# Three loads of x in an output projection, asked for earlier in SyncE's queue

## Chip, cores and metric

The kernel runs on one core of a Trainium2 chip. What is measured is the device time of one execution in microseconds. Engines are named as in the profile: PE is TensorE's matmuls, DVE is VectorE, ACT is ScalarE, POOL is GpSimd, SP is SyncE, which issues most of the DMAs.

## What is computed

One layer of a trunk, for a sequence of 512 tokens and a width of 2048, all in float32. Cut to what matters:

```python
hn = rmsnorm(x, norm_g)
y  = swa_mixer(hn, ...)               # q, k, v, gate = hn @ w_in; attention in a window of 128
                                      # returns (out * silu(gate)) @ w_out   <- the output projection
x  = x + y
g  = sigmoid(rmsnorm(x, ple_norm) @ ple_gate)
x  = x + (p @ ple_proj) * g
return rmsnorm(x, final_g)
```

## The kernel before

**Stages.** The kernel first makes the norm, the keys, the values and the first queries, then projects the remaining queries and gates while attention runs block by block, then does the output projection (`w_out`, 2048 x 2048), and last the projection by `ple_gate` with the final norm and the stores. Every float32 product is made of three matmuls on split operands (`mm3`, L126 to L128): high times high, low times high, high times low, where a high part is a cast (`fp32r`) and a low part is what the cast left over.

**The output projection** is done in Strassen-like products of quarters of the matrices. `ORDER_OUT = (1, 7, 6, 5, 3, 4)` gives the order of the six large products (the seventh is replaced by products half their size, the `small` ones). Each product `p` has two halves `jj`, for the two column blocks of 512; each half is one call of `unit` and has four steps, and a step takes one weight piece of 128 x 1024 (512 KB) and makes 2 x 2 x 3 = 12 matmuls of 128 x 512 with it. Products 1, 6, 5 and 3 add up in the same PSUM banks, so that product 1's result has to be taken out before product 6 goes on in them.

A step looks like this: `unit` gets its piece, issues its matmuls, runs some of the work queued in `later` (adds of finished products to x), then calls `todo`, which is where loads of x are asked for:

```python
def load_x(j, queue):                                                    # L1015
    queue.dma_start(x1[j], a["x"].rearrange("(t p) d -> p t d", p=P)[:, :, j * 512 : (j + 1) * 512])
...
for m in range(4):                                                       # in unit
    bh, bl = B.get(at[p, jj][m])
    ...                                                                  # 12 matmuls
    some_later(4 - m)
    todo()
...
def todo():                                                              # in the loop over ORDER_OUT
    step = next(calls)
    part = x_at.get((p, jj, step))
    if part is not None:
        load_x(part, nc.sync)
    next(nxt, None)
```

**x.** `x1s` is a tile of 128 x 4 x 4 x 512, and `x1[j]` is its part for the columns from 512 j on: 1 MB each, in rows of 2 KB (a weight piece's rows have 4 KB). Part 0 is loaded by POOL's queue just ahead of the projection; parts 2, 1 and 3 are asked for on SP's queue at the places that `x_at` names as (product, half, step): part. The tile lies in room that attention used, so the first load from each queue waits for attention's last product on PE. `add_to_x` (L1054 adds, L1056 subtracts) takes a block of 128 x 512 from PSUM and needs the x part there: product 1's halves go to parts 0 and 1, product 7's first half to parts 2 and 0, its second half to 3 and 1. Product 1's two results are held back (`waiting`) into product 7's first and product 6's first half, ahead of product 6's next use of the same banks.

**Weight pieces.** `Pieces` (the object `B`) holds the order of all pieces of this projection and the next. `ahead` asks for a piece three or four pieces before its turn (`_prepare`, L747, on SP's queue) and splits it two before its turn: the cast on ACT (L754, `bhi`) and the subtraction on DVE (L755, `blo`). A piece goes into one of three buffers (tag `wraw`), and so its load waits on SP until DVE has split the piece three before it. From product 6 on (`far_from` to `far_to`) pieces go instead into a pool of eight buffers and are asked for six pieces ahead, so that they enter SP's queue among the last pieces of product 7. The split parts have three buffers too, so that a cast waits until PE has let go of the piece three before it.

**Forms.** The activations' quarters are added, subtracted and split for the next product while the present one runs (`steps`, one step at each `todo`): `gate<-gate,gate` at L855 on DVE, `fho` at L862 and L867 on ACT, `flo` at L863 and L868 on DVE. They read the gates, not x.

**Order.** On PE and SP instructions stand in the order of the program. On DVE, ACT and POOL, in this stage, a scheduler orders them when the kernel is built, by its own estimate of when each can run. Each queue then runs strictly in order: an instruction that waits holds up all that stand behind it on its engine. SP's queue carries every load named here except x's part 0.

Of the kernel before, what the change touches and what calls it, by code (L numbers as in the profile page):

```python
# [55 lines left out]
def trunk_kernel(ctx: ExitStack, tc: tile.TileContext, a: dict):  # L56
# [958 lines left out]
    def load_x(j, queue):  # L1015
        queue.dma_start(x1[j], a["x"].rearrange("(t p) d -> p t d", p=P)[:, :, j * 512 : (j + 1) * 512])
# [128 lines left out]


    load_x(0, nc.gpsimd)
    x_at = {(1, 1, 1): 2, (7, 0, 1): 1, (7, 0, 3): 3}
    waiting = {(7, 0): (1, 0), (6, 0): (1, 1)}
    held = {}  # L1150
    for n, p in enumerate(ORDER_OUT):
# [386 lines left out]
```

## Time and profile before

| | |
|---|---|
| timed runs | 791.11, 791.59, 791.53 us; median 791.53 us |
| profiled execution | 792.39 us, its span 790.7 us |
| granted clock of TensorE | 0.998 |
| instructions | 11096 |
| loads of x: 3 on SP's queue, 1 on POOL's | 1024.0 KB each, issued at 462.55, 473.49, 479.71 us (SP) and 450.94 us (POOL) |
| loads of weight pieces of the projection from `in_w_out` and `w_out` on SP's queue | 22 + 32 of 512.0 KB |
| projection's first large product begins | 450.82 us |

Times inside an execution are in microseconds from the span's start. A row of the timeline gives start, length, engine, source line, operation, tiles (written <- read) and, in brackets, how long the engine stood idle before it and what ended that. The length of a DMA's row is the time to issue it; its transfer ends at the landing, which the view of DMA issues tells. A row of the windows gives, for a stretch, its length, busy time and instructions of PE, PE's weight loads, DVE, ACT and POOL, then the granted clock, the busy share of the 16 DMA engines and GB/s. A row of the waits gives total us, times and the longest.

### The profile page before, as it was taken

The numbers are of one execution on the slowest core, as the hardware profiler recorded it, in microseconds if no ns is written. First come the engines' busy times: TensorE is split into PE (matmuls) and PEld (weight loads), VectorE is DVE, ScalarE is ACT, GpSimd is POOL, SyncE is SP. The second block draws the span as 40 slices with busy tenths as digits, with TensorE's granted clock in tenths as the row PEclk, the third lists the DMA queues.
The fourth block names the chain that finished last, engine by engine and source line by source line (L and its number), as shares of the span: only waits on it lengthen the run. The fifth ranks groups of instructions, "written<-read, shape, count | busy, mean of one in ns | idle before, by whom it ended". The sixth has DMA issues, their size and how long they took to land. (4 is left out here: it accounts for less than half of the span.)

```text
span 790.7 us, 11096 instructions
## 1 busy us (share of the span) xinstructions
PE 779.7 (99%) x3726; PEld 652.3 (82%) x3726; DVE 607.9 (77%) x1038; ACT 506.5 (64%) x1064; POOL 137.5 (17%) x256
## 2 busy tenths in 40 slices
PE   9999999999999999999999999999999999999995
PEld 8888888888888888888888887888888888888885
DVE  4537697877878687877777897778779589877996
ACT  6733586666767576766657753457689766656953
POOL 0201423131223223122222100000000022202000
PEclk9999999999999999999999999999999999999999
DMA  9988999999999989999997579667873799989723
GB/s 348 277 216 297 194 269 300 291 289 260 282 273 262 271 238 306 263 280 262 281 270 188 142 262 377 234 210 227 269 278 101 278 300 268 240 236 253 213 96 118
DMA packets 47817, 198.07 MB, mean 251 GB/s; under 512 B 7104, under 2 KB 8128, under 8 KB 42000
## 3 DMA queue, kind: packets, MB, share of 16 engines
q1 hardware_dynamic: 38736, 151.95, 55.7%
q0 software_dynamic: 9024, 45.41, 29.6%
q8 instruction: 29, 0.48, 0.2%
q14 instruction: 28, 0.23, 0.1%
HBM read 189.16 MB, written 71.35 MB: 329 GB/s over the span
## 5 line engine op out<-in xcount | busy, mean ns | idle before, releaser
L755 DVE TENSOR_TENSOR blo<-braw,bhi 128x1024 fp32r<-128x1024 f32 x108 | 131.2, 1221 | 38.4 <-ACT bhi L754 37.6
L754 ACT CAST bhi<-braw 128x1024 fp32r<-128x1024 f32 x108 | 113.2, 1051 | 58.3 <-PE o L128 25.2
L126 PE MATMUL gps<-xh,whi 128*128 128x512 f32 x256 | 100.0, 390 | 0.0
L127 PE MATMUL gps<-xl,whi 128*128 128x512 f32 x256 | 99.9, 390 | 0.0
L128 PE MATMUL gps<-xh,wlo 128*128 128x512 f32 x256 | 99.7, 390 | 0.0
L126 PE MATMUL qps<-xh,whi 128*128 128x512 f32 x224 | 87.8, 392 | 0.0
L127 PE MATMUL qps<-xl,whi 128*128 128x512 f32 x224 | 87.4, 390 | 0.0
L128 PE MATMUL qps<-xh,wlo 128*128 128x512 f32 x224 | 87.3, 390 | 0.0
L110 DVE TENSOR_TENSOR wlo<-wraw,whi 128x1024 fp32r<-128x1024 f32 x60 | 73.5, 1227 | 3.8 <-ACT whi L109 3.6
L126 PE MATMUL o<-bhi,fho 128*128 128x512 f32 x192 | 74.9, 390 | 1.1 <-ACT bhi L754 1.1
L127 PE MATMUL o<-blo,fho 128*128 128x512 f32 x192 | 74.9, 390 | 0.8 <-DVE blo L755 0.8
L570 POOL TENSOR_SCALAR_AFFINE_SELECT own<-r 64x512 fp32r<-64x512 f32 (+1 forms) x48 | 32.4, 675 | 244.1 <-DVE r L560 240.1
L128 PE MATMUL o<-bhi,flo 128*128 128x512 f32 x192 | 74.8, 390 | 0.0
L556 ACT CAST r<-pt 128x256 fp32r<-128x256 f32 x64 | 23.9, 374 | 68.9 <-PE pt L551 68.6
L109 ACT CAST whi<-wraw 128x1024 fp32r<-128x1024 f32 x60 | 62.3, 1039 | 5.5 <-issue 4.1
L126 PE MATMUL g<-bhi,fhg 128*128 128x512 f32 x160 | 62.8, 392 | 0.0
L128 PE MATMUL g<-bhi,flg 128*128 128x512 f32 x160 | 62.3, 389 | 0.0
L127 PE MATMUL g<-blo,fhg 128*128 128x512 f32 x160 | 62.3, 389 | 0.0
L128 PEld LDWEIGHTS gps<-xh,wlo 128*128 128x128 f32 x256 | 48.1, 188 | 10.3
L126 PEld LDWEIGHTS gps<-xh,whi 128*128 128x128 f32 x256 | 48.1, 188 | 9.2
L127 PEld LDWEIGHTS gps<-xl,whi 128*128 128x128 f32 x256 | 48.1, 188 | 8.8
L529 ACT ACTIVATE t<-t,sm 128x129 f32<-128x129 f32 (+1 forms) x128 | 49.6, 389 | 8.7 <-DVE sm L525 7.4
(241 smaller groups left out, 1761.6 us busy)
## 6 DMA issues: line engine op xcount, KB each, us to landing
wraw<-in_w_gate_in SPq DMA_DIRECT2D x32, 512.0 KB, 8.1
w_out<-in_w_out POOLq DMA_DIRECT2D x32, 512.0 KB, 9.1
braw<-w_out SPq DMA_DIRECT2D x32, 512.0 KB, 4.7
wraw<-in_w_q SPq DMA_DIRECT2D x28, 512.0 KB, 6.6
braw<-in_w_out SPq DMA_DIRECT2D x22, 512.0 KB, 3.9
braw<-in_ple_gate SPq DMA_DIRECT2D x22, 512.0 KB, 5.5
xw<-in_first SPq DMA_DIRECT2D x14, 640.5 KB, 6.6
w_out<-in_w_out SPq DMA_DIRECT2D x16, 512.0 KB, 10.5
```

The costliest lines, as they stand in the source:

```text
L109: nc.scalar.copy(hi, raw)
L110: nc.vector.tensor_sub(lo, raw, hi.bitcast(F32))
L126: nc.tensor.matmul(ps, sh, mh, start=first, stop=False, skip_group_check=more)
L127: nc.tensor.matmul(ps, sh, ml, start=False, stop=False, skip_group_check=more)
L128: nc.tensor.matmul(ps, sl, mh, start=False, stop=last, skip_group_check=more)
L529: nc.scalar.activation(su, su, AF.Exp, bias=sm[:, u : u + 1], accum_out=sm[:, 2 + u : 3 + u])
L556: nc.scalar.copy(rh, src)
L570: nc.gpsimd.affine_select(out=flat(own), in_=flat(r).bitcast(F32), pattern=[[0, 8], [sign, HB]], compare_op=ALU.is_ge, fill=0.0, base=-HB ...
L754: nc.scalar.copy(hi, raw)
L755: nc.vector.tensor_sub(lo, raw, hi.bitcast(F32))
```

## The change

The places at which x's parts are asked for. Part 2 moves from the second step of product 1's second half to the last step of its first half; part 1 from the second step of product 7's first half to the second step of product 1's second half; part 3 from the fourth step of product 7's first half to the first step of the same half. Nothing else in the source is touched; the scheduler orders some instructions of DVE and ACT anew.

```diff
     load_x(0, nc.gpsimd)
-    x_at = {(1, 1, 1): 2, (7, 0, 1): 1, (7, 0, 3): 3}
+    x_at = {(1, 0, 3): 2, (1, 1, 1): 1, (7, 0, 0): 3}
     waiting = {(7, 0): (1, 0), (6, 0): (1, 1)}
```

## The prediction

> **What bounds the kernel now.** The page comes first, then the view of waits kept to PE, then PE's timeline around the wait that it names.
>
> ```profile
> span 790.7 us, 11096 instructions
> PE 779.7 (99%) x3726; PEld 652.3 (82%) x3726; DVE 607.9 (77%) x1038; ACT 506.5 (64%) x1064; POOL 137.5 (17%) x256
> ```
> ```profile
> PE o L126 <- ACT bhi L754: 1.1, 1, 1.1
> ...
> PE o L127 <- DVE blo L755: 0.8, 1, 0.8
> ```
> ```profile
> 782.51 0.39 DVE L1225 TENSOR_TENSOR s<-e,s 128x224 f32<-128x224 f32 x1 [1.15 <-PE e L128]
> ```
>
> TensorE is busy from its first to its last instruction. Behind its end stands only a tail that starts from its last product (the last row: VectorE waits for PE). In the whole span PE waits for another engine twice, both times in the output projection (tile `o`), once each for the two halves of a split weight piece. So the time can fall by little more than these waits, and any new wait of PE is paid in full. Where they stand:
>
> ```profile
> 450.82 0.40 PE L126 MATMUL o<-bhi,fho 128*128 128x512 f32 x1
> ...
> 472.84 0.39 PE L127 MATMUL o<-blo,fho 128*128 128x512 f32 x1
> ...
> 483.49 0.39 PE L126 MATMUL o<-bhi,fho 128*128 128x512 f32 x1
> ...
> 492.94 0.50 PE L126 MATMUL o<-bhi,fho 128*128 128x512 f32 x1 [1.09 <-ACT bhi L754]
> 494.20 0.50 PE L127 MATMUL o<-blo,fho 128*128 128x512 f32 x1 [0.76 <-DVE blo L755]
> ...
> 496.86 0.39 PE L126 MATMUL o<-bhi,fho 128*128 128x512 f32 x1
> ```
>
> I number the weight pieces of the projection from 0: product 1 uses 0 to 7, product 7 uses 8 to 15, product 6 starts with 16. Piece 0 begins at 450.82 and piece 12 at 483.49, so a piece costs PE 32.67 / 12 = 2.7225 us. Without a wait piece 15 would begin at 483.49 + 3 x 2.7225 = 491.66 and piece 16 at 494.38. They begin at 492.94 and 496.86. The loss is 496.86 - 494.38 = 2.48 us, all of it at piece 15 (the two waits, 1.09 and 0.76, leave out the refilling of the matmul pipe around them).
>
> Why piece 15 was late is read from the queue of SP, the landings and the two engines that split a piece:
>
> ```profile
> 425.56 34.07 SPq L747 DMA_DIRECT2D braw<-in_w_out  x8
> 462.18 0.33 SPq L747 DMA_DIRECT2D braw<-w_out  x1
> 462.55 0.43 SPq L1016 DMA_DIRECT2D x1s<-in_x  x1
> 465.64 7.80 SPq L747 DMA_DIRECT2D braw<-w_out  x4
> 473.49 0.43 SPq L1016 DMA_DIRECT2D x1s<-in_x  x1
> 476.00 3.67 SPq L747 DMA_DIRECT2D braw<-w_out  x4
> 479.71 0.43 SPq L1016 DMA_DIRECT2D x1s<-in_x  x1
> 483.21 13.55 SPq L747 DMA_DIRECT2D braw<-w_out  x9
> ```
> ```profile
> 481.36 0.69 DVE L1056 TENSOR_TENSOR x1s<-x1s,o 128x512 f32<-128x512 f32 x1 [1.91 <-DMA x1s<-in_x]
> 481.96 1.22 DVE L755 TENSOR_TENSOR blo<-braw,bhi 128x1024 fp32r<-128x1024 f32 x1
> ```
> ```profile
> 478.74 1.05 ACT L754 CAST bhi<-braw 128x1024 fp32r<-128x1024 f32 x1 [2.15 <-DMA braw<-w_out]
> ...
> 491.84 2.94 ACT L754 CAST bhi<-braw 128x1024 fp32r<-128x1024 f32 x3 [2.31 <-DMA braw<-w_out]
> ```
>
> The first of the nine at 483.21 is piece 15. It goes into one of three raw buffers and waits until DVE has split piece 12, which ends at 481.96 + 1.22 = 483.18. That split stood behind an add to x (L1056), for which DVE waited 1.91 us until x's second part had landed. Then the load itself is slow. In the views of DMA issues kept to one issue each (at 457.57, 462.55, 465.64, 473.49, 479.71 and 483.21; KB and us to landing at the end):
>
> ```profile
> braw<-in_w_out SPq DMA_DIRECT2D x1, 512.0 KB, 3.3
> ```
> ```profile
> x1s<-in_x SPq DMA_DIRECT2D x1, 1024.0 KB, 5.8
> ```
> ```profile
> braw<-w_out SPq DMA_DIRECT2D x1, 512.0 KB, 4.0
> ```
> ```profile
> x1s<-in_x SPq DMA_DIRECT2D x1, 1024.0 KB, 7.8
> ```
> ```profile
> x1s<-in_x SPq DMA_DIRECT2D x1, 1024.0 KB, 10.8
> ```
> ```profile
> braw<-w_out SPq DMA_DIRECT2D x1, 512.0 KB, 8.5
> ```
>
> Piece 15 takes 8.5 us where a piece alone takes 3.3, and lands at 491.7; its cast starts at 491.84 and PE gets it at 492.94. The windows, one for each half product, say why (DMA share and GB/s at the end):
>
> ```profile
> 461.70:472.60 10.90, 10.90 (x49) 9.01 (x48) 10.90 (x13) 5.80 (x8) 0.00 (x0) 1.00 0.77 271
> 472.60:483.50 10.90, 10.90 (x50) 9.02 (x49) 8.99 (x11) 4.46 (x5) 0.00 (x0) 1.00 0.94 333
> 483.50:494.40 10.90, 9.05 (x39) 6.96 (x38) 7.81 (x11) 5.01 (x7) 0.00 (x0) 1.00 1.03 406
> ```
>
> In the last one the 16 DMA engines are full at 406 GB/s; in the first they are not. At 406 GB/s one part of x (1.05 MB) costs 2.6 us and a piece (0.52 MB) 1.3 us. A piece alone takes 3.3, so 2.0 us of a load are latency.
>
> **The change, part by part.** The number of instructions stays; no engine gets an operation more. Three issues move up SP's queue. In the built order they stand so (pieces by number, x parts by column index): before `8, x2, 9, 10, 11, 12, x1, 13, 16, 14, 17, x3, 15, 18...`; after `6, x2, 7, 8, x1, 9, 10, 11, x3, 12, 13, 16, 14, 17, 15, 18...`.
>
> ```profile
> 457.57 0.33 SPq L747 DMA_DIRECT2D braw<-in_w_out  x1
> ```
> ```profile
> 471.39 0.32 SPq L747 DMA_DIRECT2D braw<-w_out  x1
> ```
>
> *x2* follows piece 6 (457.57): asked for at 457.9, not 462.55. It is the first of the three to enter room that attention used; the last attention product ended just ahead of 450.82, where the projection begins, so SP has nothing to wait for there. *x1* follows piece 8 (462.18): 462.55, not 473.49. *x3* follows piece 11 (471.39): 471.8, not 479.71. An issue itself costs 0.43 us of SP, which mostly waits for buffers: nothing.
>
> *What now stands behind an x.* Piece 7 follows x2, pieces 8 and 9 follow x2 and x1. Moving data from 457.57 + 2.0 = 459.6 on, at the full rate, pieces 6, x2 and 7 (2.1 MB, 5.2 us) are in by 464.8, then 8 by 466.1, x1 by 468.7 and 9 by 470.0. The row of 4.0 us at 465.64 is the same case in the trace: piece 9, 3.1 us behind an x part, landed 0.7 us later than a piece alone, at 469.6. What the landings may cost is read from DVE, which is full in this stretch (10.90 of 10.90 us):
>
> ```profile
> 470.14 1.22 DVE L755 TENSOR_TENSOR blo<-braw,bhi 128x1024 fp32r<-128x1024 f32 x1
> ...
> 471.88 1.21 DVE L755 TENSOR_TENSOR blo<-braw,bhi 128x1024 fp32r<-128x1024 f32 x1
> 473.02 1.22 DVE L855 TENSOR_TENSOR gate<-gate,gate 128x1024 f32<-128x1024 f32 x1
> ```
>
> These are the splits of pieces 8 and 9 and a form's subtraction. Piece 8 is ready at 471.36, PE's use of its low half is at 472.84: 1.5 us to spare. Its cast (1.05 us) must start by 469.1 to keep DVE's slot; landing at 466.1 leaves 3 us. Cost: nothing, cover 3 us.
>
> *The scheduler's order on DVE.* Built with the new order, the subtraction (L855) goes ahead of piece 9's split, and the two adds of product 1's second half (L1056) go ahead of piece 11's. Piece 9's split moves from 471.88 to about 473.0 and ends at 474.2; PE needs it at 450.82 + 9 x 2.72 + 0.23 = 475.5. 1.3 us are left, so nothing is paid. Piece 12 waits for that buffer: its issue slips from about 473.1 to 474.3, behind x3. Piece 11, x3 and 12 are 2.1 MB or 5.2 us from 473.4: piece 12 lands at 478.6, as now (its cast began at 478.74).
>
> *The wait that goes.* The adds need x1, which lands by 469 instead of 481.3 (473.49 + 7.8). DVE's 1.91 us wait goes. DVE was free for piece 12 at 481.36 - 1.91 = 479.45; with both adds now ahead of it (0.60 us apart by the rows at 481.36 and 481.96) it is split from 480.65 to 481.87, and piece 15 is asked for 1.3 us earlier, at 481.9. In front of it in the queue only pieces 14 and 17 are still moving (1.05 MB, 2.6 us), no x: it lands by about 485.2, the time of a piece alone. Its cast cannot begin before PE has let go of piece 12's buffer at 486.2; cast and split then end at about 488.7, 3 us ahead of its use at 491.9. Next late is nothing: behind 496.86 PE waits nowhere, and each later load there is released by a split that moves with PE.
>
> The sum: -2.48 us, nothing added. The profiled execution took 792.39 us (its span 790.7), and would take 789.9; the timed runs have a median of 791.53, 0.86 less, and give 791.53 - 2.48 = **789.05**. If all of those 0.86 us lay in this stall, the timed runs lose only 1.6 there and the result is 789.9; 788.7 if the timed runs scatter downwards as they do now (0.4 us).
>
> **The rivals.** 0.2% is 1.58 us, about what a measurement can tell from no change: from 789.95 to 793.11.
>
> *Part of the stall stays.* Right behind piece 15 SP asks for eight pieces far ahead (18 on). If the engines share their time between loads instead of serving them in order, these still slow it, and it gains only its 1.3 us of earlier issue: a stall of 1.2 us is left, 790.25. Against: in the full stretch x3, asked for at 479.71, landed at 490.5 and piece 15, 3.5 us behind it in the queue, 1.2 us later, one piece's time. Chance 0.13.
>
> *The change doesn't reach it.* The burst alone makes the stall, x or not: 791.5. Against: 1.05 MB less in a stretch that moved 406 x 10.9 = 4.4 MB. Chance 0.05.
>
> *Slower: x ahead of weights in the tight stretch.* Place: piece 9, behind x2 and x1. From 459.6 on 4.2 MB must be in by 473.1 (cast and split 2.3 us, use at 475.5), which takes 311 GB/s; below that PE waits. The trace shows 271 in that stretch. At 271 piece 9 lands at 475.1, it is split by 477.4 and PE loses 1.9 us; x3 takes 3.9 us at that rate, of which pieces 9 to 11 win back 3 x 0.8 (1.9 us each against PE's 2.72), so that piece 12 costs 1.5 more; and with the queue then as full as now at 491 the old stall stays: 791.53 + 3.4 = 794.9. For it: x's rows are shorter in memory than a piece's. Against: 271 was what was asked for (share 0.77), and the 406 came with an x part in flight. The Trainium skill, "DMA: Bandwidth & Descriptors", section "Queues, rings and completion order", says that each DMA engine takes a ring's descriptors in order, and that completion all the same isn't first in, first out. By that a piece behind an x waits out all of it (2.6 us), as in my sum; the 4.0 us row agrees, being late and not overtaking. Chance 0.09.
>
> **How the numbers follow.** Stall gone 0.73 (788.7 to 789.9), part of it 0.13, no effect 0.05, slower 0.09. The range 788.7 to 791.0 takes in the first two. Faster 0.73, same 0.13 + 0.05 = 0.18, slower 0.09.
>
> **What would show it.** Right: no wait of PE at piece 15, piece 16 beginning near 494.4, no wait of DVE for x at L1056, landings under 5 us for piece 15. Wrong: a PE wait between 464 and 484 at piece 7, 8, 9 or 12 (x in front of weights), or piece 15's cast still beginning after 489.

## The result, and the profile after

| | before | changed |
|---|---|---|
| timed runs, median | 791.27 us (790.53 to 792.31, 18 runs) | 789.87 us (789.61 to 790.63, 18 runs) |
| ratio | | 0.9983, 95% interval 0.9976 to 0.9991 |
| profiled execution, its span | 792.39 us, 790.7 | 790.63 us, 788.9 |

The changed kernel is faster by 0.17%, 1.4 us in the medians, where 2.48 us were forecast (789.05; range 788.7 to 791.0). That is a little less than the 0.2% that the prediction took as the least to be told from no change; the interval does not reach 1, so the gain is told from none all the same. The ratios here and below are on record with their intervals; they are not the quotients of the medians and can differ from these by up to 0.001. The profile after, the page and then the waits of PE:

```profile
span 788.9 us, 11095 instructions
PE 779.8 (99%) x3726; PEld 652.7 (83%) x3726; DVE 608.1 (77%) x1038; ACT 507.1 (64%) x1064; POOL 138.8 (18%) x256
```
```profile
PE warm_ps L141 <- PEq L1528: 0.8, 1, 0.8
```

Both waits in the projection are gone; the one left is the program's start. In PE's timeline these are the first matmuls of pieces 0, 15 and 16:

```profile
451.35 0.40 PE L126 MATMUL o<-bhi,fho 128*128 128x512 f32 x1
...
492.17 0.39 PE L126 MATMUL o<-bhi,fho 128*128 128x512 f32 x1
...
494.89 0.39 PE L126 MATMUL o<-bhi,fho 128*128 128x512 f32 x1
```

From piece 0 to piece 16 it is 494.89 - 451.35 = 43.54 us, before 496.86 - 450.82 = 46.04: in these two executions 2.50 us came from exactly where the prediction put 2.48. The spans differ by only 1.8 because this execution reached the projection 0.53 us later, in code that the change doesn't touch, and took 294.0 instead of 293.8 us behind piece 16.

How the loads now stand in SP's queue; then, on DVE, the split of piece 9, the two adds and the split of piece 12; then, on ACT, the casts of pieces 12 and 15:

```profile
458.46 0.43 SPq L1016 DMA_DIRECT2D x1s<-in_x  x1
459.82 0.33 SPq L747 DMA_DIRECT2D braw<-in_w_out  x1
462.69 0.33 SPq L747 DMA_DIRECT2D braw<-w_out  x1
463.07 0.43 SPq L1016 DMA_DIRECT2D x1s<-in_x  x1
466.16 6.07 SPq L747 DMA_DIRECT2D braw<-w_out  x3
472.28 0.43 SPq L1016 DMA_DIRECT2D x1s<-in_x  x1
```
```profile
473.53 1.22 DVE L755 TENSOR_TENSOR blo<-braw,bhi 128x1024 fp32r<-128x1024 f32 x1
...
476.40 1.28 DVE L1056 TENSOR_TENSOR x1s<-x1s,o 128x512 f32<-128x512 f32 x2
...
481.55 1.23 DVE L755 TENSOR_TENSOR blo<-braw,bhi 128x1024 fp32r<-128x1024 f32 x1 [0.39 <-ACT bhi L754]
```
```profile
480.46 1.06 ACT L754 CAST bhi<-braw 128x1024 fp32r<-128x1024 f32 x1 [2.90 <-DMA braw<-w_out]
...
488.77 1.05 ACT L754 CAST bhi<-braw 128x1024 fp32r<-128x1024 f32 x1 [1.44 <-DMA braw<-w_out]
```

The two adds no longer wait; piece 12 is split late only because its own load landed late; piece 15's cast still waits for its load, but at 488.77 and not at 491.84. The loads of piece 9 (issued at 466.16) and piece 15 (at 482.81), each from the view of DMA issues kept to that one:

```profile
braw<-w_out SPq DMA_DIRECT2D x1, 512.0 KB, 5.9
```

Both took 5.9 us, 9 instead of 4.0 and 15 instead of 8.5. (The load of piece 9 varies by itself: in two more profiles of the kernel before, taken below, it took 5.2 and 5.9 us.) The windows show the full stretch spread over the three half products:

```profile
461.70:472.60 10.90, 10.90 (x50) 9.03 (x49) 10.90 (x13) 5.37 (x7) 0.00 (x0) 1.00 0.93 351
472.60:483.50 10.90, 10.90 (x50) 9.03 (x49) 10.31 (x12) 5.26 (x6) 0.00 (x0) 1.00 0.98 351
483.50:494.40 10.90, 10.90 (x49) 9.03 (x49) 9.13 (x12) 5.76 (x7) 0.00 (x0) 1.00 0.99 377
```

271, 333 and 406 GB/s have become 351, 351 and 377.

### The profile page after: what moved, and what is told of

It is laid out like the page before. It is cut to its first block, busy times and chain, and to the rows that moved or that the text cites. A ratio compares the mean times of both kernels' runs of the same rounds, so it can differ in the third digit from the quotient of the medians.

```text
span 788.9 us, 11095 instructions
## 1 busy us (share of the span) xinstructions
PE 779.8 (99%) x3726; PEld 652.7 (83%) x3726; DVE 608.1 (77%) x1038; ACT 507.1 (64%) x1064; POOL 138.8 (18%) x256
## 5 line engine op out<-in xcount | busy, mean ns | idle before, releaser
L560 DVE TENSOR_TENSOR r<-pt,r 128x256 fp32r<-128x256 f32 x56 | 23.7, 423 | 41.0 <-ACT r L556 40.4
```

Source lines behind the costliest of these rows:

```text
L560: nc.vector.tensor_sub(rl, src, rh.bitcast(F32))
```

## The experiments

Two questions were open. Which of the two things that the prediction took together made piece 15 late: that it was asked for late, behind adds that waited for x's part 1, or that part 3's megabyte stood in front of it? And why do the medians differ by 1.4 us when the profiles show 2.5 us of wait? Each experiment stands beside runs of the kernel before on its own chip; there were three such chips, on which the kernel before has medians of 791.1, 790.49 and 790.9 us.

**The kernel before, profiled again (`b_again`, `b_third`).** No edit.

> The kernel before, unchanged, for a second profile. Open is why the profiles differ by 2.5 us at piece 15 while the medians differ by 1.4 us. Theory A (the wait differs from execution to execution and the first profile caught a long one): the wait at piece 15 is again there but of another size, anywhere from 0.5 to 2.5 us, and the span moves with it. Theory B (the wait is always 2.5 us, and the changed kernel loses 1.1 us somewhere else): 2.4 to 2.6 us again, span 790.5 to 791.

> The kernel before, unchanged, for a third profile: the first had 2.5 us of loss at piece 15, the second 1.9. If the wait differs from execution to execution, a third value between 0.5 and 2.5; if it is a matter of the profile alone, 1.9 to 2.5 again.

PE at piece 15 in the second and in the third profile:

```profile
492.69 0.49 PE L126 MATMUL o<-bhi,fho 128*128 128x512 f32 x1 [0.56 <-ACT bhi L754]
493.95 0.50 PE L127 MATMUL o<-blo,fho 128*128 128x512 f32 x1 [0.77 <-DVE blo L755]
```
```profile
491.53 0.50 PE L126 MATMUL o<-bhi,fho 128*128 128x512 f32 x1
492.79 0.50 PE L127 MATMUL o<-blo,fho 128*128 128x512 f32 x1 [0.76 <-DVE blo L755]
```

Measured as in the prediction, against the pitch of pieces 0 to 12, the loss is 1.9 us in the second (span 790.4) and 1.3 us in the third (span 789.3), 2.5 in the first. The wait is there in all three and each time of another size, and the three spans follow it. The runs of the kernel before spread from 789.87 to 793.24 us over all comparisons here; a part of that is not the wait, since the projection itself began between 450.47 and 451.35 us in the profiles of all kernels. So the gain isn't a constant of the change either, but the size of a wait that differs from execution to execution.

The landings tell where the difference arises. They are counted here from piece 0's first matmul. Piece 17, the last load in front of part 3, landed after 36.95, 36.40 and 35.78 us in the three profiles, and piece 15 after 40.94, 40.37 and 39.76, each time 4.0 us later: 2.7 for part 3 and 1.3 for itself. The loss is in all three the landing of piece 15 less 38.46 us, within 0.03 us. So the price of part 3 is the same each time; what differs is how far the queue has come by then. Why that differs is not shown.

**Part 1 alone (`x1_alone`).**

```diff
-    x_at = {(1, 1, 1): 2, (7, 0, 1): 1, (7, 0, 3): 3}
+    x_at = {(1, 1, 1): 2, (1, 1, 2): 1, (7, 0, 3): 3}
```

> Only part 1 moves: asked for right behind piece 9 (466.0 instead of 473.5), so that the two adds do not wait for it; part 3 stays in the queue in front of piece 15. If the late asking for piece 15 (behind the adds that waited for part 1) is what counts, the wait at piece 15 falls to 0 to 0.5 us and the time to that of the changed kernel (ratio 0.998 to 0.9985). If the megabyte of part 3 in front of piece 15 is what counts, at least 1.2 us of the wait stay and the ratio is 0.9992 or more.

791.65 us against 791.1, ratio 1.0008 (0.9999 to 1.0016). The adds no longer wait for part 1, and piece 15 is asked for at 481.71, 1.5 us before the time in the first profile. It gains nothing by it:

```profile
braw<-w_out SPq DMA_DIRECT2D x1, 512.0 KB, 10.4
```

It took 10.4 us instead of 8.5 and landed at 492.1 (before: 491.7), since part 3 was still ahead of it and the engines were full. In this full queue, asking earlier was not landing earlier. The edit did one thing more, though: in DVE's new order the two adds stand ahead of piece 10's split, so that piece 13, which goes into that buffer, was asked for at 477.70 instead of 476.00 (1.2 us later, counted from piece 0), and the DMA engines were not full in the stretch before:

```profile
472.60:483.50 10.90, 10.90 (x50) 9.03 (x49) 10.34 (x12) 4.84 (x5) 0.00 (x0) 1.00 0.80 261
```

So this run shows that the earlier asking doesn't suffice, and not what part 1's megabyte is worth. In this execution the wait was also followed by something that the prediction did not know of, told at the end.

**Part 3 alone, moved back (`x3_behind`).**

```diff
-    x_at = {(1, 1, 1): 2, (7, 0, 1): 1, (7, 0, 3): 3}
+    x_at = {(1, 1, 1): 2, (7, 0, 1): 1, (7, 1, 0): 3}
```

> Only part 3 moves, and it moves back, not forward: behind pieces 15 and 18 in SP's queue. The adds wait for part 1 as before (1.9 us) and piece 15 is asked for at 483.2 as before; DVE's order is that of before. If the megabyte in front of piece 15 counts, it lands 2.6 us earlier, near 489.2, and the wait at piece 15 falls to 0 to 0.4 us (ratio 0.998 to 0.9987). If the late asking counts, most of the wait stays: over 1.2 us, ratio 0.9992 or more.

790.07 us against 791.1, ratio 0.9983 (0.9974 to 0.9992): the same ratio as the change, with parts 1 and 2 at their old places. DVE's order is that of before up to piece 14's split; piece 15's split then stands one step earlier, ahead of a form's low part. That can't have made the gain, as in the kernel before DVE stood idle for 2.2 us ahead of piece 15's split. PE waits nowhere in the projection. The adds still wait for part 1, if less than in the first profile (0.8 us instead of 1.9), and piece 15 is asked for at 482.58. Counted from piece 0 that is 1.1 us earlier than in the first profile, and 0.9 us later than in `x1_alone`, where the earlier asking gained nothing. Here are the add, the load of piece 15 (asked for at 482.58) and its cast:

```profile
480.73 0.69 DVE L1056 TENSOR_TENSOR x1s<-x1s,o 128x512 f32<-128x512 f32 x1 [0.81 <-DMA x1s<-in_x]
```
```profile
braw<-w_out SPq DMA_DIRECT2D x1, 512.0 KB, 5.1
```
```profile
487.82 1.05 ACT L754 CAST bhi<-braw 128x1024 fp32r<-128x1024 f32 x1 [0.54 <-DMA braw<-w_out]
```

It landed at 487.7, now 1.3 us behind piece 17 and not 4.0. Its cast begins at 487.82, 1 us before that of the changed kernel. The megabyte in front of piece 15 decides.

**Part 3 alone, moved forward (`x3_alone`).**

```diff
-    x_at = {(1, 1, 1): 2, (7, 0, 1): 1, (7, 0, 3): 3}
+    x_at = {(1, 1, 1): 2, (7, 0, 0): 3, (7, 0, 1): 1}
```

> Only part 3 moves forward, behind piece 11 as in the changed kernel; parts 2 and 1 stay. No x is left between pieces 14 and 15 in the queue, but part 1 now stands behind part 3 and piece 12 and should land near 483.5; the two adds, which DVE here has behind piece 12's split, wait for it and hold up piece 13's split. Theory 'the bytes in front of piece 15': no wait at piece 15; a small one of 0.3 to 0.8 us at piece 13; ratio 0.9985 to 0.9995. Theory 'the late asking behind the adds': the adds wait longer than before, so the wait at piece 15 stays or grows; ratio 1.000 or more.

790.01 us against 790.49, ratio 0.9993 (0.9984 to 1.0002): the times alone don't tell this from no change. The profile has no wait of PE, at 13 neither: part 1 landed at 481.5, two us sooner than expected, and DVE waited 0.3 us for it. But piece 15 has almost nothing in hand:

```profile
490.67 2.36 DVE L755 TENSOR_TENSOR blo<-braw,bhi 128x1024 fp32r<-128x1024 f32 x2 [0.25 <-ACT bhi L754]
```

The first of the two is piece 15's split. It ends at 490.67 + 1.22 = 491.9, and PE uses it at 492.1, 0.2 us later. With part 3 forward and parts 2 and 1 where they were, the engines are full from 472.6 on (390 GB/s, then 408), and everything behind is just in time. The other two moves, into the stretch with room, bring the reserve of the changed kernel, 1.3 us in its first profile and 1.9 in a second one (`a_again`).

**Part 2 alone (`x2_alone`).**

```diff
-    x_at = {(1, 1, 1): 2, (7, 0, 1): 1, (7, 0, 3): 3}
+    x_at = {(1, 0, 3): 2, (7, 0, 1): 1, (7, 0, 3): 3}
```

> Only part 2 moves, into a stretch in which the DMA engines have time, and far ahead of the full stretch. Expected by both theories: nothing, the wait at piece 15 stays at 1.3 to 2.5 us; ratio 0.9993 to 1.0007. If the part of the gain that the prediction could not place lies with part 2, the ratio is 0.999 or less.

790.61 us against 790.49, ratio 0.9997 (0.9988 to 1.0006). No gain that could be measured; but the times on this chip could hardly have shown one, as `x3_alone`, in whose profile PE's wait is gone, measured 0.9993 there. The wait stays. In the profiled execution the loss is 0.6 us, less than expected and less than in the three profiles of the kernel before; whether that is the move or one more draw, a single profile doesn't tell:

```profile
491.98 0.50 PE L127 MATMUL o<-blo,fho 128*128 128x512 f32 x1 [0.29 <-DVE blo L755]
```

**One more megabyte (`one_more`).** It loads data that the computation doesn't need.

```diff
                 if part is not None:
                     load_x(part, nc.sync)
+                    if part == 3:
+                        nc.sync.dma_start(
+                            fg.rearrange("p (t d) -> p t d", t=4),
+                            a["x"].rearrange("(t p) d -> p t d", p=P)[:, :, 3 * 512 :],
+                        )
```

> As before, with one more load of 1 MB (part 3 of x once more, into a tile that is not in use yet and is overwritten later) right behind part 3 and ahead of piece 15. If loads are served in the queue's order at 406 GB/s, piece 15 lands 2.6 us later and the wait grows from 2.5 to about 5.1 us in the profile. For the timed runs: if the profile shows the wait as the timed runs have it, the time grows by 2.6 us (ratio 1.0033); if timed runs have a shorter wait of 1.4 us than the profile's 2.5 by a smaller load on the DMA engines, it grows by clearly less, 1.5 to 2 us (ratio 1.002 to 1.0025).

796.44 us (794.51 to 796.65), ratio 1.0057 (1.0045 to 1.0069): 5.3 us between the medians (4.5 by the ratio) for 1 MB, where a megabyte takes 2.6 us at the full rate, and more than either reading allowed. The profiled execution (794.84 us) shows the wait, then the granted clock in three windows around and behind it:

```profile
493.91 0.50 PE L126 MATMUL o<-bhi,fho 128*128 128x512 f32 x1 [2.42 <-ACT bhi L754]
495.17 0.50 PE L127 MATMUL o<-blo,fho 128*128 128x512 f32 x1 [0.76 <-DVE blo L755]
...
496.44 0.63 PE L128 MATMUL o<-bhi,flo 128*128 128x512 f32 x1
```
```profile
491.00:495.00 4.00, 0.99 (x4) 0.25 (x2) 1.80 (x2) 2.81 (x4) 0.00 (x0) 1.00 1.02 409
495.00:499.00 4.00, 3.83 (x11) 3.01 (x11) 2.99 (x5) 0.75 (x1) 0.00 (x0) 0.61 1.03 410
499.00:503.00 4.00, 4.00 (x18) 3.34 (x17) 3.43 (x6) 2.27 (x3) 0.00 (x0) 0.96 0.54 210
```

Here piece 16 begins 5.3 us late (499.38; at the pitch from piece 14's start at 488.60 it would be 494.05), of which about 1.5 us are matmuls at half rate (worked out at the end) and 3.8 the wait itself. The landings show that the megabyte by itself cost what was expected: it landed 2.7 us behind part 3, and piece 15 landed 6.7 us behind piece 17 where it was 4.0 before. An estimate from these numbers: without it the wait of this execution would have been 3.8 - 2.7 = 1.1 us, and the rest of its price is the slower clock. The question about timed runs that this kernel should have answered it does not answer: three of the four other runs lie 1.6 us or more above the profiled one, and what they added can't be seen.

**All three parts ahead of piece 9 (`x_earlier`).**

```diff
-    x_at = {(1, 1, 1): 2, (7, 0, 1): 1, (7, 0, 3): 3}
+    x_at = {(1, 0, 3): 2, (1, 1, 0): 1, (1, 1, 1): 3}
```

> All three parts ahead of piece 9: behind pieces 6, 7 and 8. This is the rival of the prediction, pushed to its place. By the rate that the changed kernel's trace shows in that stretch (351 GB/s, piece 9 landed at 472.1) piece 9 lands 1.05 MB or 3 us later, near 475, and is ready near 477.3 where PE wants it at 476.1: a wait of 1 to 1.5 us at piece 9, none at piece 15; ratio 0.9995 to 1.000, and 1.002 if the granted clock falls behind the wait as in two of the kernels before. If the engines serve the three parts beside the pieces without delaying them, no wait anywhere and a ratio of 0.998 to 0.9985.

792.09 us against 790.49, ratio 1.002 (1.0011 to 1.0029): slower, at the place of the prediction's third rival, but not by its mechanism. Piece 9 was asked for at 465.31 and took 7.4 us: it landed at 472.8, not near 475, because the engines moved 401 GB/s there. PE waited all the same, at a granted clock of 1.00, and DVE's row of work tells why:

```profile
477.49 0.51 PE L127 MATMUL o<-blo,fho 128*128 128x512 f32 x1 [1.66 <-DVE blo L755]
```
```profile
472.68 0.68 DVE L1056 TENSOR_TENSOR x1s<-x1s,o 128x512 f32<-128x512 f32 x1
473.28 0.68 DVE L868 TENSOR_TENSOR flo<-gate,fho 128x512 fp32r<-128x512 f32 x1
473.88 0.68 DVE L1056 TENSOR_TENSOR x1s<-x1s,o 128x512 f32<-128x512 f32 x1
474.48 0.68 DVE L1091 TENSOR_TENSOR small_sums_o<-gate 128x512 f32<-128x512 f32 x1
475.08 1.22 DVE L855 TENSOR_TENSOR gate<-gate,gate 128x1024 f32<-128x1024 f32 x1
476.22 2.35 DVE L755 TENSOR_TENSOR blo<-braw,bhi 128x1024 fp32r<-128x1024 f32 x2
```

The cast of piece 9 ended at 473.9; its split began at 476.22. The scheduler, which orders DVE by its own estimate of when each instruction can run, had put an add and two other steps between, and DVE was never idle. Split at 473.9, piece 9 would have been ready at 475.1, before PE's use at 475.7. The loss is 1.9 us at piece 9 and 0.4 at piece 8.

**The changed kernel on another chip, and with part 3 behind piece 15 (`a_again`, `both`).**

The edit is that of `both`, against the changed kernel; `a_again` has none.

```diff
-    x_at = {(1, 0, 3): 2, (1, 1, 1): 1, (7, 0, 0): 3}
+    x_at = {(1, 0, 3): 2, (1, 1, 1): 1, (7, 1, 0): 3}
```

> The changed kernel once more, on another chip. If its gain is the wait of the kernel before and that differs from chip to chip and run to run, its own time stays near 789.9 us (its profile without a wait at piece 15, 1 us or more in hand), while the ratio follows the time of before: 0.9975 to 0.9995. If the changed kernel has a wait of its own in some executions, its times spread as widely as those of before (2 us or more).

> The changed kernel with part 3 behind pieces 15 and 18 instead of behind piece 11: parts 2 and 1 early, no x between 14 and 15. The likeliest version to be better, with the most in hand at piece 15 (2 to 3 us against 1.3) and at piece 12. If no wait is left in the changed kernel, there is nothing to win: the same time within 0.3 us. If the timed runs of the changed kernel still hold a rest of the wait, this one is faster by up to 0.5 us and its times spread less.

The changed kernel: 789.74 us (789.58 to 790.26) against 790.9 (790.13 to 792.47), ratio 0.9985 (0.9976 to 0.9994). With part 3 behind: 789.81 us (789.54 to 790.25), ratio 0.9991 (0.9982 to 1.0). Both profiles are without a wait, and the times are the same; piece 15 has 1.9 us in hand in the one and 2.9 in the other. Once the wait was gone, more reserve bought nothing that could be measured. The changed kernel's runs spread over 0.7 us, those of the kernel before beside them over 2.3.

## Why the prediction was right, and where it missed

*What bounds the kernel* held: PE's wait at piece 15 went and the time fell; no other wait came in its place.

*The sum's one term* was mis-sized: 2.48 us, read from a single execution, against 1.40 us between the medians here and 1.16 on the other chip. Of three profiles of the kernel before, the one read was the longest: 2.5, 1.9 and 1.3 us, with executions of 792.39, 792.12 and 791.03 us. The prediction saw the sign of this, the profiled execution being 0.86 us above the median, and gave 789.9 as the bound if all of that lay in the stall; 789.87 was measured. It should have taken that bound's side as its middle. That 789.05 missed by only 0.82 us is in part luck: the gain was put 1.08 us too large, and the median of three runs that it was taken from, 791.53, lay 0.26 above that of eighteen. How long the wait is in a timed run is not seen by anything here. An estimate from the profiles: a run takes 1.7 us more than its span, and the span less the projection's start and less the loss is 337.3 to 337.6 us in the profiles at full clock; with the projection starting between 450.47 and 451.35, a run at the median of 791.27 has a loss of 0.6 to 1.8 us.

*"The wait that goes"* named two causes and joined them. The wait of the adds did go, but it was not what made piece 15 late: `x1_alone` took it away and kept PE's wait; `x3_behind` kept 0.8 us of it and lost PE's wait. What counts is the clause that there is "no x" in front of piece 15: in the six profiles in which part 3 stands between pieces 17 and 15, piece 15 landed 4.0 us behind piece 17 (6.7 in `one_more`, with two megabytes), and in five of the six others 1.3 us (2.5 in the changed kernel's first).

*Piece 15's landing* was put at "the time of a piece alone", 3.3 us, with landings under 5 us as a sign of being right; it took 5.9 and landed at 488.7, about 3 us later than forecast when the later start of 0.53 us is allowed for. The cover was the 3 us in hand, of which 1.3 were left. The step that failed is the queue in front of it. The prediction had only pieces 14 and 17 still moving; piece 16 was moving too when 15 was asked for at 482.81 (it landed at 483.24), 17 landed at 486.19, and 15 came 2.5 us behind it. The rate was a part of this: the sum moved everything at 406 GB/s, and from the asking to the landing of piece 15 the engines moved 375. (The 351 of the first two windows above is lower still, as these take in gaps in which little was asked for.) Why it came 2.5 us behind piece 17, and only 1.3 in `a_again` and `both`, is open.

*Piece 9* was forecast in by 470.0 (470.5 with the later start) and landed at 472.1; from 459.5 until then the engines moved 368 GB/s. Its cast ended 0.3 us before DVE came to its split, so that the cover was nearly used up there. But the "same case in the trace" was one draw too: counted from piece 0, piece 9 landed after 18.8, 20.0 and 20.8 us in the three profiles of the kernel before, of which the prediction had read the first, and after 20.7 us in the changed kernel.

*The scheduler's order on DVE* held to a tenth: piece 9's split ended at 474.75 (474.2 plus the later start), 1.3 us ahead of PE's use, as worked out.

*The rivals.* "Part of the stall stays" and "the change doesn't reach it" are out: no wait was left in either profile of the changed kernel. The ground of the first, that the engines might share their time between loads instead of serving them in order, is not borne out either: in all twelve traces the loads on SP's queue landed in the order in which they were asked for, from piece 0's first matmul to 46 us behind it. The slower one has its place right, piece 9, as `x_earlier` shows, but its price there came through DVE's order and not through the landings. That a piece behind an x waits out all of it, as the prediction read the Trainium skill, "DMA: Bandwidth & Descriptors", section "Queues, rings and completion order", agrees with the 2.7 us of part 3.

## What to carry to other kernels

In a queue that was full, as here, a load's place decided when it landed: look for what large transfer stands in front of the one that the bounding engine needs next, and move it into a stretch in which the DMA engines have room, or behind. A wait that one profile shows is one draw: where the timed runs spread over more than the change is worth, price it by several profiles before forecasting its removal. And where a scheduler orders an engine by its own estimates, moving a load moves instructions too: read the new order against that engine's spare time.

## What the hardware showed that was not expected

A short wait of PE can cost more than its length. In `x1_alone` PE issued one matmul between 491.94 and 494.56 us; from then until 497.97, for 3.4 us, matmuls started 0.43 us apart instead of 0.23, and the windows show the granted clock:

```profile
494.56 0.62 PE L127 MATMUL o<-blo,fho 128*128 128x512 f32 x1 [0.76 <-DVE blo L755]
494.98 0.63 PE L128 MATMUL o<-bhi,flo 128*128 128x512 f32 x1
```
```profile
491.00:495.00 4.00, 2.27 (x9) 1.27 (x8) 1.78 (x3) 2.79 (x4) 0.00 (x0) 0.97 1.03 410
495.00:499.00 4.00, 4.00 (x12) 3.19 (x11) 3.17 (x5) 0.91 (x2) 0.00 (x0) 0.60 0.94 336
499.00:503.00 4.00, 4.00 (x19) 3.29 (x18) 3.09 (x5) 2.37 (x3) 0.00 (x0) 1.00 0.50 148
```

Piece 16 began 3.9 us late. The matmuls from 494.56 up to it, at 498.79, took 4.23 us; in the first profile of the kernel before, the same ones took 2.66 (494.20 to 496.86). So 1.6 us of the loss are the slower clock, on top of a wait of 2.3. In `one_more` the same stretch took 4.21 us, 495.17 to 499.38, and so cost 1.55 us more. The kernel before, in its first profile, had the same gap, 491.46 to 494.20 with one matmul in it, 0.1 us longer, and kept its clock:

```profile
495.00:499.00 4.00, 4.00 (x19) 3.28 (x18) 3.82 (x6) 1.87 (x3) 0.00 (x0) 1.00 0.96 315
```

`one_more`, with a gap of 4.1 us, lost its clock for 3.4 us too. The Trainium skill, "TensorE: Matmul & The Clock Gate", Part 1 on the clock gate, says that half rate comes after at least one idle window of some 3.4 us, and that the window runs freely. The 3.4 us for which the matmuls ran slower have the length of such a window. But a gap of 2.6 us with a matmul in it is shorter than an idle window, so the rule as stated doesn't cover `x1_alone`, and the measurement decides: such a gap was enough. That one of 2.7 us was not would fit a free-running window better than a fixed threshold, but no run here settles it. If timed runs of the kernel before meet it now and then, that would add to their spread; this was not shown either.
